# Strassen's seven products for 17 of the 22 pairs of a feed-forward sublayer, in a one-core fp32 block

## The chip, the core and the metric

The kernel runs on one core of a Trainium2 chip, in a single launch. The metric is the device time of that launch in microseconds (us). TensorE (PE in the profile) does the matrix products, VectorE (DVE) and ScalarE (ACT) the elementwise work, GpSimd (POOL) a little of it, and SyncE (SP) issues the DMAs. TensorE's clock has two levels, 1.2 and 2.4 GHz; the profile shows the granted one as a share of the upper.

## The reference

A block of three sublayers on 512 tokens of width 1024, in fp32: a feed-forward sublayer, a mixer of pooling and state-space parts, and a second feed-forward sublayer. Each normalizes its input, modulates it by vectors made from `c`, and adds its gated result to `x`. The change is in the second feed-forward sublayer, whose reference is, cut to what matters (`D_FF` is 2816):

```
def swiglu(h, w_in, w_out):
    a, b = jnp.split(h @ w_in, 2, axis=-1)
    return (jax.nn.silu(a) * b) @ w_out

h = modulate(rmsnorm(x, norm_g[layer, 2]), shift[:, 2], scale[:, 2])
x = x + FFN_RES_WEIGHT * gate[:, 2, None, :] * swiglu(h, ffn2_in[layer], ffn2_out[layer])
return rmsnorm(x, final_g)
```

## The kernel before

**Precision.** An fp32 operand is held as two fp32r tiles, a high part `hi` (a cast) and the rest `lo` (source minus `hi`). A product of two operands is three matmuls into one PSUM bank: hi by hi, hi by lo, lo by hi (`mm3`, L310 to L312). Activations lie with features on the 128 partitions and the 512 tokens along the free dimension, so an operand `h` of 1024 features is 8 such tiles, k = 0 to 7.

**Weights.** They stream from HBM in units of 128 x 1024 (512 KB). For each unit `Weights.load` has SP issue a DMA into a tile `w_raw` (RAW = 3 of them), ScalarE casts it to `w_hi` (L121) and VectorE subtracts to get `w_lo` (L124), in rings of RING = 5 tiles. `fill` asks for the splits of AHEAD = 3 units beyond the one in use. So a cast takes a buffer that TensorE has just finished with, the subtraction follows the cast, and a `w_raw` tile is free for the next DMA after the subtraction.

**A feed-forward sublayer.** The 2816 hidden features are 22 pairs: pair i is the 128 features i of `a` and the 128 of `b`. `pair` makes both products, 8 k each, 512 tokens wide: 48 matmuls of 512 columns. `glu` then takes silu of the first on ScalarE (L524), multiplies by the second on VectorE (L526), and `split` makes the hi and lo tiles (L323 on ScalarE, L325 on VectorE). The pairs come in portions, (0, 8), (8, 16) and (16, 22); after each portion the 8 output products (128 output features each, over the portion's pairs as k) are run and added to `x` by VectorE (`add_out`, L443). Of the last portion two output products are 512 wide and the other six are done in two halves of 256 tokens (`out_halves`), so that the final norm can begin on one half. The first two pairs are made in halves too (`in_halves`). After the last pair come the out products and the final norm.

**Order.** TensorE's order is the program's order, written by hand. The Tile scheduler orders the other engines within the dependencies, and each engine then runs its instructions strictly in the order that it was given. PSUM has 8 banks of 512 fp32, all from one pool, and a wait for a bank is for the whole tile.

**The modulation vectors.** Rows of `w_ada` (512 KB each, tile `row`, 4 of them) are loaded and reduced on VectorE in the first feed-forward sublayer and its start, L391 and L402.

Of the kernel before, what the change touches and what calls it, by code (L numbers as in the profile page):

```python
# [8 lines left out]
F32 = mybir.dt.float32  # L9
# [8 lines left out]
HT = 256  # L18
KD = 8
NPAIR = 22  # L20
PORTIONS = ((0, 8), (8, 16), (16, 22))
NHEAD = 24
NG = 4
NCHK = 4
EPS = 1e-5
NSTART = 4
# [12 lines left out]
WARM = 24  # L39
WARM1 = 7  # L40
# [42 lines left out]
class Weights:  # L83


    def __init__(self, nc, pool, units, big):
        self.nc, self.pool, self.units, self.big = nc, pool, units, big
        self.raw, self.split = [], []
        self.first, self.ring = [0], [0]
        for _, count, _, extra in units:  # L90
            self.first.append(self.first[-1] + count)
            self.ring.append(self.ring[-1] + (not extra))
        self.at = self.done = 0
        self.unit = -1
        self.auto = False

    def load(self, upto):
        while len(self.raw) < min(upto, len(self.units)):
            ap, count, width, _ = self.units[len(self.raw)]
            raw = self.pool.tile([P, KD * P], F32, name="w_raw", tag="w_raw", bufs=RAW)  # L100
            self.nc.sync.dma_start(out=raw[:, :count * width], in_=ap)
            self.raw.append(raw)

    def ensure(self, upto, between=None):
        nc = self.nc
        while len(self.split) < min(upto, len(self.units)):
            i = len(self.split)
            _, count, width, extra = self.units[i]
            self.load(i + 1)
            raw, self.raw[i] = self.raw[i], None  # L110
            parts = []
            step = NT if extra else KD * P
            for c in range(0, count * width, step):
                n = min(step, count * width - c)
                if extra:
# [4 lines left out]
                r = raw[:, c:c + n]  # L120
                nc.scalar.copy(out=hi[:, :n], in_=r)  # L121
                if between:
                    between()
                nc.vector.tensor_tensor(out=lo[:, :n], in0=r, in1=hi[:, :n].bitcast(F32), op=ALU.subtract)  # L124
                parts += [(hi[:, j:j + width], lo[:, j:j + width]) for j in range(0, n, width)]
            self.split.append(parts)

    def fill(self, more=0):

        if not self.auto:  # L130
            return
        used = max(u for u in range(len(self.units) + 1) if self.first[u] <= self.done)
        want = min(self.unit + 1 + AHEAD + more, len(self.units))
        while len(self.split) < want and self.ring[len(self.split) + 1] - self.ring[used] <= RING:
            self.ensure(len(self.split) + 1)
        self.load(min(self.unit + AHEAD + RAW + more, len(self.split) + RAW))

    def next(self, hold=False):

# [96 lines left out]
class Block:  # L236
# [25 lines left out]

    def plan(self):
        a = self.a
        u = [(a["w1s"][k], 2 * NSTART, P, False) for k in range(KD)]
# [7 lines left out]
        def ffn(f, first):  # L273
            for pi, (p0, p1) in enumerate(PORTIONS):
                for t in range(2 * max(p0, first), 2 * p1):
                    u.append((a["ffn%d_in" % f][t], KD, P, False))
                stream(a["ffn%d_out%d" % (f, pi)])

        def halves(ap):
            u.extend((ap[i], KD, P, True) for i in range(4))  # L280

        ffn(1, NSTART)
# [7 lines left out]
        ffn(2, 2)  # L290
        return u

    @staticmethod
    def mixer_order():
# [6 lines left out]
                + [("outB", m) for m in range(MLATE)])  # L301


    def mm3(self, ps, w, act, sl, first, last):
# [5 lines left out]
        T.matmul(o, lhsT=hi, rhs=ahi[:, s], start=first, stop=False)  # L310
        T.matmul(o, lhsT=hi, rhs=alo[:, s], start=False, stop=False)  # L311
        T.matmul(o, lhsT=lo, rhs=ahi[:, s], start=False, stop=last)  # L312

    def product(self, ps, ws, acts, sl=FULL, mid=None):
        for k, act in enumerate(acts):
            if mid:
                mid(k / len(acts))
            self.mm3(ps, ws[k] if ws else self.W.next(), act, sl, k == 0, k == len(acts) - 1)

    def split(self, src, hi, lo, sl=FULL, pool=False):  # L320
        s = slice(*sl)
# [63 lines left out]
        self.accumulate(acc[:, s], q)  # L385


    def ada_load(self, j, k):

        w = self.sb.tile([P, KD * P], F32, name="row", tag="row", bufs=NROW)  # L390
        self.nc.sync.dma_start(out=w, in_=self.a["ada"][j, k])  # L391
        return w

    def ada_sum(self, j, k, w):

# [9 lines left out]
    def ada_rest(self):  # L405

        steps = [(j, k) for j in (2, 4, 3, 5, 7, 6, 8) for k in range(KD)]
        ws = []
        for i, (j, k) in enumerate(steps):
            ws += [self.ada_load(*t) for t in steps[len(ws):i + NROW]]  # L410
            self.ada_sum(j, k, ws[i])
            yield

# [119 lines left out]
        self.product(pb, None, h)  # L533
        self.glu(pa, pb, FULL, g)

    def ffn(self, h, gs, j, gate, norm, late, spread, pumps=(0, 0)):
        for pi, (p0, p1) in enumerate(PORTIONS):
            if pi:
                gs = {i: self.new_act() for i in range(p0, p1)}
            for i in range(max(p0, j), p1):  # L540
                self.pair(h, gs[i])
                self.pump(pumps[0])
            acts = [gs[i] for i in range(p0, p1)]
            last = pi == len(PORTIONS) - 1
            for m in range(late if last else KD):
                self.out_full(m, acts, gate, last)()
                self.pump(pumps[1])
            if last:
                self.pump(1000)
                norm = norm()  # L550
                for m in range(late):
                    norm.scale(m)
                self.out_halves(range(late, KD), acts, gate, norm, spread)


    def start(self):
# [4 lines left out]
    def first_pairs(self):  # L561
# [33 lines left out]

        def load(k):
            if k < KD:
                rows[k] = [self.ada_load(j, k) for j in (1, 0)]
            self.W.load(k + 1)

        for k in range(2):
# [57 lines left out]
        pss = [self.bank() for _ in range(2 * NSTART)]  # L659
        T = nc.tensor  # L660
        for k in range(KD):
            load(k + 2)
            ws = self.W.take(2 * NSTART)
            if k == 0:
                for n, (a, b) in enumerate(((0, 0), (1, 0), (0, 1))):
                    for w, p in zip(ws, pss):
# [9 lines left out]
                self.W.ensure(k + 4)  # L676
        self.W.auto = True
        a = self.a
        gs = {j: self.new_act() for j in range(*PORTIONS[0])}
        for j in range(NSTART):  # L680
# [365 lines left out]
def arrange(inputs):  # L1046
# [61 lines left out]
```

## Time and profile before

| | |
|---|---|
| median of 3 runs | 1138.57 us (1135.80 to 1139.15) |
| the profiled execution | 1137.97 us |
| its span, first to last instruction | 1136.2 us |
| mean granted TensorE clock | 0.996 |
| TensorE busy | 1126.4 us, 99% |
| VectorE busy | 635.6 us, 56% |
| ScalarE busy | 391.2 us, 34% |
| GpSimd busy | 117.3 us, 10% |
| DMA moved | 140.61 MB, 124 GB/s over the span |

The chain of waits is followed back from the last instruction; an engine that holds nearly all of it sets the time. The second feed-forward sublayer runs from about 764 us to the end; pairs 2 to 21 with their output products lie between 780 and 1097 us. A busy share tells how full an engine is, but not whether it hands over late: that is read from single instructions, by their start, their length and what ended the idle time before them. Matmuls are pipelined, so the pace of a stream is the distance of their starts, not the length shown for one.

### The profile page before, as it was taken

The numbers are of one execution on the slowest core, as the hardware profiler recorded it, in microseconds if no ns is written. First come the engines' busy times: TensorE is split into PE (matmuls) and PEld (weight loads), VectorE is DVE, ScalarE is ACT, GpSimd is POOL, SyncE is SP. The second block draws the span as 40 slices with busy tenths as digits, with TensorE's granted clock in tenths as the row PEclk, the third lists the DMA queues.
The fourth block names the chain that finished last, engine by engine and source line by source line (L and its number), as shares of the span: only waits on it lengthen the run. The fifth ranks groups of instructions, "written<-read, shape, count | busy, mean of one in ns | idle before, by whom it ended". The sixth has DMA issues, their size and how long they took to land.

```text
span 1136.2 us, 14273 instructions
## 1 busy us (share of the span) xinstructions
PE 1126.4 (99%) x5708; PEld 937.9 (83%) x5708; DVE 635.6 (56%) x969; ACT 391.2 (34%) x632; POOL 117.3 (10%) x122
## 2 busy tenths in 40 slices
PE   8999999999999999999999999999999999999997
PEld 8888888888888988888888878899888888888887
DVE  6998887333335747778777685563333333333334
ACT  4442122221224534444454452443221222212232
POOL 0000000000000410122302660121000000000011
PEclk8999999999999999999999999999999999999999
DMA  8898986332234302121213123420332223323302
GB/s 323 305 324 319 328 324 250 93 93 93 92 93 132 98 32 90 60 88 62 75 56 89 42 75 93 148 94 21 97 102 97 93 93 93 93 94 94 101 28 74
DMA packets 39954, 140.61 MB, mean 124 GB/s; under 512 B 4432, under 2 KB 5840, under 8 KB 39888
## 3 DMA queue, kind: packets, MB, share of 16 engines
q1 hardware_dynamic: 39888, 139.71, 37.0%
q8 instruction: 44, 0.72, 0.3%
q14 instruction: 22, 0.18, 0.0%
HBM read 137.60 MB, written 2.10 MB: 123 GB/s over the span
## 4 chain that ended last, share of the span: by engine, by line
PE 98%; DMA 1%; DVE 1%; SPq 0%; issue 0%; DVEq 0%
PE ps_mm L311 24%; PE ps_mm L310 24%; PE ps_mm L312 24%; PE ps_t L311 6%; PE ps_t L312 6%; PE ps_t L310 6%; PE ps_y L887 1%; PE ps_mm L373 1%; PE ps_t L881 1%; PE ps_y L906 1%; PE ps_mm L350 1%; DMA row<-in_ada_dram 1%; PE ps_mm L667 1%; PE ps_t L849 0%; PE ps_t L854 0%; PE ps_t L852 0%
## 5 line engine op out<-in xcount | busy, mean ns | idle before, releaser
L310 PE MATMUL ps_mm<-big,w_hi 128*128 128x512 f32 (+1 forms) x1198 | 451.8, 377 | 0.0
L311 PE MATMUL ps_mm<-big,w_hi 128*128 128x512 f32 (+1 forms) x1198 | 450.1, 376 | 0.0
L312 PE MATMUL ps_mm<-big,w_lo 128*128 128x512 f32 (+1 forms) x1198 | 450.0, 376 | 0.0
L121 ACT CAST w_hi<-w_raw 128x1024 fp32r<-128x1024 f32 x176 | 185.0, 1052 | 515.2 <-PE ps_mm L311 341.4
L124 DVE TENSOR_TENSOR w_lo<-w_raw,w_hi 128x1024 fp32r<-128x1024 f32 x176 | 220.2, 1252 | 169.4 <-ACT w_hi L121 159.4
L310 PEld LDWEIGHTS ps_mm<-big,w_hi 128*128 128x128 f32 x1198 | 225.1, 188 | 46.9 <-issue 2.9
L311 PEld LDWEIGHTS ps_mm<-big,w_hi 128*128 128x128 f32 x1198 | 225.5, 188 | 45.2 <-issue 0.7
L312 PEld LDWEIGHTS ps_mm<-big,w_lo 128*128 128x128 f32 x1198 | 224.9, 188 | 42.7
L311 PE MATMUL ps_t<-big,w_hi 128*128 128x512 f32 x304 | 120.2, 395 | 0.0
L312 PE MATMUL ps_t<-big,w_lo 128*128 128x512 f32 x304 | 120.1, 395 | 0.0
L443 DVE SCALAR_TENSOR_TENSOR x<-ps_mm,mod,x 128x512 f32<-128x512 f32 (+1 forms) x79 | 51.0, 647 | 122.6 <-PE ps_mm L312 122.6
L310 PE MATMUL ps_t<-big,w_hi 128*128 128x512 f32 x304 | 119.0, 391 | 0.0
L329 POOL TENSOR_TENSOR sacc<-sacc,sq 128x256 f32<-128x256 f32 (+1 forms) x30 | 28.6, 953 | 729.4 <-ACT sq L384 399.5
L526 DVE TENSOR_TENSOR tmp<-tmp,ps_t 128x512 f32<-128x512 f32 x38 | 26.1, 687 | 112.9 <-PE ps_t L312 112.9
L310 PEld LDWEIGHTS ps_t<-big,w_hi 128*128 128x128 f32 x304 | 57.0, 188 | 14.0
L311 PEld LDWEIGHTS ps_t<-big,w_hi 128*128 128x128 f32 x304 | 57.0, 188 | 13.9
L312 PEld LDWEIGHTS ps_t<-big,w_lo 128*128 128x128 f32 x304 | 57.1, 188 | 12.7
L799 DVE SCALAR_TENSOR_TENSOR big<-ps_mm,vec,big 128x511 f32<-128x511 f32 (+2 forms) x60 | 44.6, 744 | 2.2 <-ACT big L797 1.3
L402 DVE CUSTOM_DVE_ANT_0 row<-row,cb,vec 128x1024 f32<-128x1024 f32 x32 | 40.3, 1279 | 2.7 <-DMA row<-in_ada_dram 2.7
L323 ACT CAST big<-tmp 128x512 fp32r<-128x512 f32 (+1 forms) x66 | 36.4, 554 | 2.5 <-DVE tmp L526 2.0
L310 PE MATMUL ps_mm<-big 128*128 128x256 f32 x128 | 36.5, 285 | 0.0
L311 PE MATMUL ps_mm<-big 128*128 128x256 f32 x128 | 36.2, 283 | 0.0
(170 smaller groups left out, 909.7 us busy)
## 6 DMA issues: line engine op xcount, KB each, us to landing
w_raw<-in_ffn_in_dram SPq DMA_DIRECT2D x76, 512.0 KB, 3.5
row<-in_ada_dram SPq DMA_DIRECT2D x72, 512.0 KB, 5.6
w_raw<-in_ffn_out_dram SPq DMA_DIRECT2D x44, 512.0 KB, 3.7
w_raw<-in_w_in_dram SPq DMA_DIRECT2D x32, 512.0 KB, 3.5
w_raw<-in_w_outB_dram SPq DMA_DIRECT2D x10, 512.0 KB, 3.4
w_raw<-in_w1s_dram SPq DMA_DIRECT2D x8, 512.0 KB, 6.6
w_raw<-in_w_outA_dram SPq DMA_DIRECT2D x6, 512.0 KB, 3.7
x<-in_x_dram SPq DMA_DIRECT2D x4, 512.0 KB, 5.3
```

What stands on the lines that cost most here:

```text
L121: nc.scalar.copy(out=hi[:, :n], in_=r)
L124: nc.vector.tensor_tensor(out=lo[:, :n], in0=r, in1=hi[:, :n].bitcast(F32), op=ALU.subtract)
L310: T.matmul(o, lhsT=hi, rhs=ahi[:, s], start=first, stop=False)
L311: T.matmul(o, lhsT=hi, rhs=alo[:, s], start=False, stop=False)
L312: T.matmul(o, lhsT=lo, rhs=ahi[:, s], start=False, stop=last)
L323: self.nc.scalar.copy(out=hi[:, s], in_=src[:, :n])
L329: self.nc.gpsimd.tensor_tensor(out=acc, in0=acc, in1=q, op=ALU.add)
L350: self.nc.tensor.matmul(ps[:, at + j:at + j + 1], lhsT=acc[:, c * P - c0:(c + 1) * P - c0], rhs=self.ones[:, 0:1], start=i == 0, stop=i == ...
L402: self.nc.vector.tensor_tensor_reduce(out=w, in0=w, in1=self.cb, scale=scale, scalar=bias, op0=ALU.mult, op1=ALU.add, accum_out=out)
L443: self.nc.vector.scalar_tensor_tensor(out=xs, in0=ps[:, :n], scalar=self.mod[:, gate, m:m + 1], in1=xs, op0=ALU.mult, op1=ALU.add)
L526: nc.vector.tensor_tensor(out=g32, in0=sa, in1=pb[:, :n], op=ALU.mult)
L799: V.scalar_tensor_tensor(out=acc[:, s:], in0=ps[:, :NT - s], scalar=tap(3 - s), in1=acc[:, s:], op0=ALU.mult, op1=ALU.add)
```

## The change

For pairs 5 to 21 of the second feed-forward sublayer the two products are made together, by a scheme with seven products in place of eight. The operand is cut in four: tokens 0 to 255 and 256 to 511 (A and B), and k = 0 to 3 and 4 to 7 (low and up). The weights of a pair are cut by k in the same way, and by `a` and `b`. Seven products of four k by 256 columns, of sums of these quarters, give the four quarter results after additions and subtractions. Such a pair (`quad`) is 84 matmuls of 256 columns.

- The sums of activations are made once, by `combine`, during pairs 2 to 4, which stay plain.
- The sums of weights are made on VectorE for each pair (`part`, L134, L135, L139), in place in a new tile `row` of 128 x 5 x 512, of which there are two. The four weight quarters come in two DMAs (768 and 256 KB, L121 and L122); what comes from the sums are three units of 1024 (U0, U1, U2) and one of 512 (U3), cast by L167 and subtracted by L170.
- A quad's products stand in nine places s1 to s9: x, y, x again, z, out product 1, x, out product 2, z, x. y and z are the two halves of one bank. ScalarE copies partial sums out (L448, L454, L456), VectorE adds what comes later (L450, L462, L466).
- The portions become (0, 4), (4, 8), (8, 12), (12, 16), (16, 22), and the output products of one portion are woven between the pairs of the next: two to a pair, and 1, 1, 2, 1, 1, 2 in the last six.
- RAW goes from 3 to 2, loads may run up to 8 units ahead, and the ada rows come two to a `row` tile.

The diff, cut to its core:

```
+PORTIONS = {1: ((0, 8), (8, 16), (16, 22)), 2: ((0, 4), (4, 8), (8, 12), (12, 16), (16, 22))}
+FIRST = {1: 4, 2: 2}
+QUADS = {1: NPAIR, 2: 5}
+WOVEN = {1: False, 2: True}
-RAW = 3
+RAW = 2
-NROW = 4
+NROW = 2
+LOADS = 8
...
+            if quad:
+                raw = self.last = self.row()
+                self.nc.sync.dma_start(out=raw[:, 2:5].rearrange("p s n -> p (s n)"), in_=ap[:, NT:])
+                self.nc.sync.dma_start(out=raw[:, 0], in_=ap[:, :NT])
...
+    def part(self, raw, kind):
+        V = self.nc.vector
+        if kind == 0:
+            return raw[:, 2::2]
+        if kind == 1:
+            V.tensor_tensor(out=raw[:, 1:4:2], in0=raw[:, 0:3:2], in1=raw[:, 3:4].broadcast_to([P, 2, NT]), op=ALU.add)
+            V.tensor_tensor(out=raw[:, 2], in0=raw[:, 1], in1=raw[:, 2], op=ALU.add)
+            return raw[:, 1:3]
+        if kind == 2:
+            return raw[:, 0:4:3]
+        V.tensor_tensor(out=raw[:, 4], in0=raw[:, 2], in1=raw[:, 4], op=ALU.add)
+        return raw[:, 4:5]
...
+    def combine(self, h):
...
+        for k in range(n):
+            wa, wb, t, u = (self.tmp() for _ in range(4))
+            for w, (hi, lo) in ((wa, h[k]), (wb, h[k + n])):
+                add(w, hi.bitcast(F32), lo.bitcast(F32), ALU.add)
+            add(t[:, la], wa[:, la], wa[:, lb], ALU.subtract)
+            less(t[:, lb], t[:, la], wb[:, lb])
+            self.t12[k] = self.new_act()
+            self.split(t, *self.t12[k])
...
+    def quad(self, h, g, outs):
...
+        x, yz = self.bank(), self.bank("t")
+        y, z = yz[:, :HT], yz[:, HT:]
+        one, two = self.tmp(), self.tmp()
+        la, lb = slice(*HALF_A), slice(*HALF_B)
+        ws = W.take(2 * n, hold=True)
+        block(x, ws[:n], low, True)
+        S.copy(out=one[:, la], in_=x[:, la])
+        block(y, ws[n:], [(act, HALF_A) for act in up], True)
+        V.tensor_tensor(out=one[:, la], in0=one[:, la], in1=y, op=ALU.add)
+        W.release(2 * n)
+        ws = W.take(2 * n, hold=True)
+        block(x, ws[n:], t2, False)
+        S.copy(out=one[:, lb], in_=x[:, la])
+        block(z, ws[:n], t1, True)
+        S.copy(out=two[:, lb], in_=z)
+        W.release(2 * n)
+        outs = outs()
+        outs[0]()
+        wb = W.take(2 * n, hold=True)
+        block(x, wb[n:], self.t3, False)
+        V.tensor_tensor(out=two[:, lb], in0=two[:, lb], in1=x[:, la], op=ALU.add)
+        outs[1]()
+        W.fill()
+        block(z, W.take(n, hold=True), [(act, HALF_B) for act in up], False)
+        V.tensor_tensor(out=one[:, lb], in0=one[:, lb], in1=z, op=ALU.add)
+        block(x, wb[:n], t4, False)
+        W.release(3 * n)
+        S.activation(out=one, in_=one, func=AF.Silu)
+        for src, c in ((two, lb), (x, la)):
+            V.scalar_tensor_tensor(out=two[:, c], in0=src[:, c], scalar=-1.0, in1=one[:, c], op0=ALU.mult, op1=ALU.mult)
+        self.split(two, *g)
...
+        self.bg = self.combine(norms[2].h)
+        self.ffn(2, norms[2].h, gs, 8, lambda: final, LATE2, SPREAD3, (2, 0))
```

On VectorE a stretch of the second portion of before reads as follows; a pair has two subtractions for its weights, its multiplication (L526) and its split (L325), and output products follow after the portion, each with its addition (L443) and a subtraction:

```order
L124 TENSOR_TENSOR w_lo<-w_raw,w_hi 128x1024
L526 TENSOR_TENSOR tmp<-tmp,ps_t 128x512
L124 TENSOR_TENSOR w_lo<-w_raw,w_hi 128x1024
L325 TENSOR_TENSOR big<-tmp,big 128x512
L443 SCALAR_TENSOR_TENSOR x<-ps_mm,mod,x 128x512
```

After the change, twelve of the sixteen VectorE rows of the step from one pair to the next (here from pair 7 to pair 8) are below; L466 and the two L471 end pair 7, the first two L170 are U2 and U3 of pair 8, L450 belongs to pair 8, then come U0 and U1 of pair 9 with L135 and L139, and L134 makes the first sums of pair 10:

```order
L466 TENSOR_TENSOR tmp<-tmp,ps_t 128x256
L170 TENSOR_TENSOR w_lo<-row,w_hi 128x1024
L471 SCALAR_TENSOR_TENSOR tmp<-tmp 128x256
L471 SCALAR_TENSOR_TENSOR tmp<-ps_mm,tmp 128x256
L170 TENSOR_TENSOR w_lo<-row,w_hi 128x512
L479 TENSOR_TENSOR big<-tmp,big 128x512
L450 TENSOR_TENSOR tmp<-tmp,ps_t 128x256
L170 TENSOR_TENSOR w_lo<-row,w_hi 128x1024
L135 TENSOR_TENSOR row<-row 128x512
L139 TENSOR_TENSOR row<-row 128x512
L170 TENSOR_TENSOR w_lo<-row,w_hi 128x1024
L134 TENSOR_TENSOR row<-row 128x2x512
```

The four rows after these are the output addition L601, L462, a second L601 and the subtraction of the out weights; then the same sixteen rows come again for the next pair. L450, which reads y, now stands behind the previous pair's L471, the subtraction of U3 and the split L479.

On TensorE, the border between the two products of pair 5 of before, with the waits of its matmuls (ps_mm is the bank of the first product, ps_t that of the second; Activation and DVE are the engines whose signal is waited for):

```order
L310 MATMUL ps_mm<-big,w_hi 128x512
L311 MATMUL ps_mm<-big,w_hi 128x512
L312 MATMUL ps_mm<-big,w_lo 128x512
L310 MATMUL ps_t<-big,w_hi 128x512 [waits Activation_49]
L311 MATMUL ps_t<-big,w_hi 128x512
L312 MATMUL ps_t<-big,w_lo 128x512 [waits DVE_49]
```

After the change the border from s3 to s4 of a quad, where z (in ps_t) follows x (in ps_mm):

```order
L381 MATMUL ps_mm<-big,w_hi 128x256
L382 MATMUL ps_mm<-big,w_hi 128x256
L383 MATMUL ps_mm<-big,w_lo 128x256
L381 MATMUL ps_t<-big,w_hi 128x256 [waits DVE_49]
L382 MATMUL ps_t<-big,w_hi 128x256
L383 MATMUL ps_t<-big,w_lo 128x256
L381 MATMUL ps_t<-big,w_hi 128x256
```

The waits of before are for the cast and the subtraction of the weights of the second product; that of the quad is for VectorE's L450, which reads the other half of the same bank.

## Rows read from the trace of the kernel before

**Rows 1.** The page: engines' busy time, and the chain that ended last.

```profile
PE 1126.4 (99%) x5708; PEld 937.9 (83%) x5708; DVE 635.6 (56%) x969; ACT 391.2 (34%) x632; POOL 117.3 (10%) x122
...
PE 98%; DMA 1%; DVE 1%; SPq 0%; issue 0%; DVEq 0%
```

**Rows 2.** Busy time by stretch: PE, PEld, DVE, ACT, POOL, clock, DMA share, GB/s.

```profile
0.00:120.00 120.00, 117.12 (x524) 96.40 (x525) 104.28 (x156) 44.82 (x57) 0.73 (x6) 0.97 0.89 320
...
900.00:1050.00 150.00, 150.00 (x651) 121.86 (x650) 51.96 (x55) 38.44 (x46) 0.00 (x0) 1.00 0.30 95
...
1098.00:1114.00 16.00, 16.00 (x131) 15.69 (x130) 4.88 (x8) 4.07 (x10) 4.96 (x6) 1.00 0.01 2
```

**Rows 3.** Groups by shape, 784 to 1097 us: busy, mean ns, idle before, releaser.

```profile
L124 DVE TENSOR_TENSOR w_lo<-w_raw,w_hi 128x1024 fp32r<-128x1024 f32 x56 | 68.6, 1225 | 81.5 <-ACT w_hi L121 77.0
...
L121 ACT CAST w_hi<-w_raw 128x1024 fp32r<-128x1024 f32 x57 | 59.9, 1051 | 231.1 <-PE ps_mm L311 151.0 <-issue 64.1 <-PE ps_t L311 16.0
...
L526 DVE TENSOR_TENSOR tmp<-tmp,ps_t 128x512 f32<-128x512 f32 x20 | 13.7, 687 | 70.2 <-PE ps_t L312 70.2
...
L325 DVE TENSOR_TENSOR big<-tmp,big 128x512 fp32r<-128x512 f32 x20 | 13.7, 683 | 0.0
...
L443 DVE SCALAR_TENSOR_TENSOR x<-ps_mm,mod,x 128x512 f32<-128x512 f32 x17 | 12.7, 750 | 55.3 <-PE ps_mm L312 55.3
...
L323 ACT CAST big<-tmp 128x512 fp32r<-128x512 f32 x20 | 12.4, 622 | 0.0
...
L524 ACT ACTIVATE tmp<-ps_mm 128x512 f32<-128x512 f32 x20 | 11.8, 592 | 0.0
```

**Rows 4.** TensorE in a pair: start us, us, engine, line, operation.

```profile
785.54 0.39 PE L310 MATMUL ps_mm<-big,w_hi 128*128 128x512 f32 x1
...
787.62 0.39 PE L310 MATMUL ps_t<-big,w_hi 128*128 128x512 f32 x1
```

**Rows 5.** TensorE's 256-column matmuls, and one weight load.

```profile
765.20 0.28 PE L310 MATMUL ps_mm<-big 128*128 128x256 f32 x1
...
780.56 0.28 PE L312 MATMUL ps_mm<-big 128*128 128x256 f32 x1
...
1099.85 0.28 PE L312 MATMUL ps_mm<-big,w_lo 128*128 128x256 f32 x1
...
1100.20 0.19 PEld L310 LDWEIGHTS ps_mm<-big,w_hi 128*128 128x128 f32 x1
...
1113.98 0.28 PE L312 MATMUL ps_mm<-big,w_lo 128*128 128x256 f32 x1
```

**Rows 6.** Groups by shape, 560 to 1136 us, 256 columns wide.

```profile
L443 DVE SCALAR_TENSOR_TENSOR x<-ps_mm,mod,x 128x256 f32<-128x256 f32 x18 | 8.7, 481 | 19.8 <-PE ps_mm L312 19.8
...
L526 DVE TENSOR_TENSOR tmp<-tmp,ps_mm 128x256 f32<-128x256 f32 x4 | 1.7, 420 | 8.7 <-ACT tmp L524 6.6 <-issue 2.1
...
L524 ACT ACTIVATE tmp<-ps_mm 128x256 f32<-128x256 f32 x4 | 1.5, 386 | 6.7 <-PE ps_mm L312 6.7
```

**Rows 7.** Single instructions: handing over between engines, and two in a row.

```profile
785.76 0.40 PE L311 MATMUL ps_mm<-big,w_hi 128*128 128x512 f32 x1
...
786.20 1.05 ACT L121 CAST w_hi<-w_raw 128x1024 fp32r<-128x1024 f32 x1 [4.39 <-PE ps_mm L311]
...
787.28 1.23 DVE L124 TENSOR_TENSOR w_lo<-w_raw,w_hi 128x1024 fp32r<-128x1024 f32 x1 [5.02 <-ACT w_hi L121]
...
903.76 1.22 DVE L124 TENSOR_TENSOR w_lo<-w_raw,w_hi 128x1024 fp32r<-128x1024 f32 x1
...
904.91 0.68 DVE L325 TENSOR_TENSOR big<-tmp,big 128x512 fp32r<-128x512 f32 x1
```

**Rows 8.** DMA issues, time to landing; last the row tile, 0 to 120 us.

```profile
w_raw<-in_ffn_in_dram SPq DMA_DIRECT2D x76, 512.0 KB, 3.5
...
out_dram<-big SPq DMA_DIRECT2D x4, 256.0 KB, 2.4
...
DMA to landing us min/median/max: 3.4/5.5/9.5
```

More of the change, by code (lines that the diff above doesn't have):

```diff
@@ L25 @@
 EPS = 1e-5
-NSTART = 4
 LATE1 = 2
@@ L107, in ensure @@
             i = len(self.split)
-            _, count, width, extra = self.units[i]
+            _, count, width, kind = self.units[i]
             self.load(i + 1)
             raw, self.raw[i] = self.raw[i], None
+            if kind in (True, False) and type(kind) is bool:
+                self.out[False] -= 1
+            else:
+                self.out[True] -= kind == 3
+                raw = self.part(raw, kind)
             parts = []
-            step = NT if extra else KD * P
+            step = NT if kind is True else KD * P
             for c in range(0, count * width, step):
                 n = min(step, count * width - c)
-                if extra:
+                if kind is True:
                     hi, lo = self.big(F32R), self.big(F32R)
@@ L135, in fill @@
             self.ensure(len(self.split) + 1)
-        self.load(min(self.unit + AHEAD + RAW + more, len(self.split) + RAW))
+        self.load(min(self.unit + AHEAD + LOADS + more, len(self.split) + LOADS))
     def next(self, hold=False):
@@ L264, in plan @@
         a = self.a
-        u = [(a["w1s"][k], 2 * NSTART, P, False) for k in range(KD)]
+        u = [(a["w1s"][k], 2 * FIRST[1], P, False) for k in range(KD)]
         def stream(ap):
@@ L271, in stream, with ffn @@
                 u.append((ap[:, t * P:e * P], e - t, P, False))
[L273 to L277, printed above, removed]
+        def ffn(f):
+            w, out = a["ffn%d_in" % f], "ffn%d_out%d"
+            for i, outs in self.steps(f):
+                if i is None:
+                    stream(a[out % (f, outs[0][0])])
+                    continue
+                ts = []
+                if outs:
+                    pi = outs[0][0]
+                    n = PORTIONS[f][pi][1] - PORTIONS[f][pi][0]
+                    m = outs[0][1]
+                    ts = [(a[out % (f, pi)][:, m * n * P:(m + len(outs)) * n * P], n * len(outs), P, False)]
+                if i < QUADS[f]:
+                    u.extend([(w[2 * i], KD, P, False), (w[2 * i + 1], KD, P, False)] + ts)
+                else:
+                    u.extend([(a["ffn%d_inQ" % f][i - QUADS[f]], KD, P, 0), (None, KD, P, 1)] + ts
+                             + [(None, KD, P, 2), (None, KD // 2, P, 3)])
+            stream(a[out % (f, len(PORTIONS[f]) - 1)])
         def halves(ap):
             u.extend((ap[i], KD, P, True) for i in range(4))
-        ffn(1, NSTART)
+        ffn(1)
         halves(a["w_inH"])
@@ L289, in plan, with steps @@
         halves(a["ffn2_inH"])
-        ffn(2, 2)
+        ffn(2)
         return u
+    @staticmethod
+    def steps(f):
+        for pi, (p0, p1) in enumerate(PORTIONS[f]):
+            pairs = range(max(p0, FIRST[f]), p1)
+            n = len(pairs)
+            for x, i in enumerate(pairs):
+                ms = range(x * KD // n, (x + 1) * KD // n) if pi and WOVEN[f] else ()
+                yield i, [(pi - 1, m) for m in ms]
+            if not WOVEN[f] and pi < len(PORTIONS[f]) - 1:
+                yield None, [(pi, m) for m in range(KD)]
     @staticmethod
@@ L301, in mixer_order, with mm3 @@
                 + [("outB", m) for m in range(MLATE)])
-    def mm3(self, ps, w, act, sl, first, last):
+    def mm3(self, ps, w, act, sl, first, last, again=False):
         hi, lo = w
@@ L318, in product, with add, less @@
             self.mm3(ps, ws[k] if ws else self.W.next(), act, sl, k == 0, k == len(acts) - 1)
+    def combine(self, h):
+        V = self.nc.vector
+        n = KD // 2
+        la, lb = slice(*HALF_A), slice(*HALF_B)
+        self.t12, self.t3 = [None] * n, [None] * n
+        last = []
+        def add(out, a, b, op):
+            V.tensor_tensor(out=out, in0=a, in1=b, op=op)
+        def less(out, a, b):
+            V.scalar_tensor_tensor(out=out, in0=a, scalar=-1.0, in1=b, op0=ALU.mult, op1=ALU.subtract)
+        for k in range(n):
[6 more added lines that the diff above has]
+            self.split(t, *self.t12[k])
+            if k % 2 == 0:
+                three, four = self.new_act(), self.big()
+            sl = (HALF_A, HALF_B)[k % 2]
+            add(u[:, la], wb[:, lb], wa[:, lb], ALU.subtract)
+            self.split(u, *three, sl)
+            self.t3[k] = three, sl
+            less(four[:, slice(*sl)], t[:, lb], wb[:, la])
+            last.append((four[:, slice(*sl)], h[k]))
+            yield
+        while self.plain:
+            yield
+        for src, act in last:
+            self.split(src, *act, HALF_B)
+        yield
@@ L385, in square_into, with ada_load @@
         self.accumulate(acc[:, s], q)
[L388 to L392, printed above, removed]
+    def ada_load(self, todo):
+        row = self.W.row().rearrange("p s n -> p (s n)")
+        ws = []
+        for i, (j, k) in enumerate(todo):
+            ws.append(row[:, i * KD * P:(i + 1) * KD * P])
+            self.nc.sync.dma_start(out=ws[i], in_=self.a["ada"][j, k])
+        return ws
     def ada_sum(self, j, k, w):
@@ L409, in ada_rest @@
         for i, (j, k) in enumerate(steps):
-            ws += [self.ada_load(*t) for t in steps[len(ws):i + NROW]]
+            while i % 2 == 0 and len(ws) < min(i + 4, len(steps)):
+                ws += self.ada_load(steps[len(ws):len(ws) + 2])
             self.ada_sum(j, k, ws[i])
@@ L534, in pair, with ffn, weights, outs @@
         self.glu(pa, pb, FULL, g)
[L536 to L540, printed above, removed]
+    def ffn(self, f, h, gs, gate, norm, late, spread, pumps=(0, 0)):
+        ports = PORTIONS[f]
+        def weights(todo):
+            return [self.W.take(ports[pi][1] - ports[pi][0], hold=True) for pi, _ in todo]
+        def outs(todo, ws=None):
+            for n, (pi, m) in enumerate(todo):
+                acts = [gs[i] for i in range(*ports[pi])]
+                ps = self.bank()
+                self.product(ps, ws[n] if ws else weights([(pi, m)])[0], acts)
+                self.W.release(len(acts), False)
+                self.add_out(ps, m, FULL, gate, False)
+                self.pump(pumps[1])
+        def halves(todo):
+            ws = weights(todo)
+            return [lambda: outs(todo[:1], ws[:1]), lambda: outs(todo[1:], ws[1:])]
+        self.plain = True
+        for i, todo in self.steps(f):
+            if i is None:
+                outs(todo)
+                continue
+            gs[i] = self.new_act()
+            if i < QUADS[f]:
                 self.pair(h, gs[i])
                 self.pump(pumps[0])
[L543 to L548, printed above, removed]
-                self.pump(1000)
[L550 to L553, printed above, removed]
+                outs(todo)
+                continue
+            if self.plain:
+                self.plain = False
+                self.pump(1000)
+            self.quad(h, gs[i], lambda: halves(todo))
+        acts = [gs[i] for i in range(*ports[-1])]
+        for m in range(late):
+            self.out_full(m, acts, gate, True)()
+            self.pump(pumps[1])
+        self.pump(1000)
+        norm = norm()
+        for m in range(late):
+            norm.scale(m)
+        self.out_halves(range(late, KD), acts, gate, norm, spread)
     def start(self):
@@ L597, in load @@
             if k < KD:
-                rows[k] = [self.ada_load(j, k) for j in (1, 0)]
+                rows[k] = self.ada_load([(1, k), (0, k)])
             self.W.load(k + 1)
@@ L657, in prepare @@
                                                   op0=ALU.add, op1=ALU.subtract)
-        pss = [self.bank() for _ in range(2 * NSTART)]
+        pss = [self.bank() for _ in range(2 * FIRST[1])]
         T = nc.tensor
```

66 lines of the change are left out of this document (46 added, 20 removed).

## The prediction

> **What bounds the kernel now.** I read the page's first part and its chain of waits, then the stretch table of the second feed-forward sublayer, then single instructions. TensorE is busy for 99% of the span and 98% of the chain is TensorE [rows 1]: time is won only by giving it less to do, as long as nothing makes it wait. In the sublayer's stretch that holds without a gap: 150.00 of 150 us at full clock (2.4 GHz), with VectorE at 52 us (35%), ScalarE at 38 and the DMA engines at 0.30 [rows 2]. VectorE and ScalarE wait for TensorE there: the cast of a weight (L121) follows the last read of the buffer it takes, the subtraction (L124) follows the cast [rows 3]. So two questions decide: how fast TensorE runs the new, smaller matmuls, and whether VectorE, which gets twice the work, still hands over in time.
>
> **TensorE's sum.** A pair now is 48 matmuls of 512 columns. From one L310 to the ninth matmul after it pass 2.08 us [rows 4], 0.2311 us each: 11.09 us a pair. A quad is 84 matmuls of 256 columns (seven products, four k, three each). Such matmuls run in two places of before: 120 steps from 1099.85 to 1113.98, 0.1178 each, twelve or more to a bank; and 128 steps from 765.20 to 780.56, 0.1200 each, with a new bank every three [rows 5]. The quad stays twelve matmuls in a bank, so I take 0.1178: 9.89 us. Bounds: 0.1200 gives 10.08, half of a 512-column step gives 9.71. A quad saves 1.20 us (1.01 to 1.38), seventeen save 20.4 us (17.2 to 23.5). The out products keep their matmuls and shapes (528 of k times m, however they are cut); the end of the sublayer is unchanged. A change between widths costs nothing by the rows: a step is as long as the matmul before it.
>
> Each matmul has its own weight load, so 17 x 36 = 612 are added. One takes 0.19 us, longer than the step it has to fit in; yet in the 256-column stretch loads start every 0.12 us beside the matmuls and the pace holds [rows 5]. I cost them at nothing. The Trainium skill ("TensorE: Matmul & The Clock Gate", "The mechanism") says that a weight load overlaps matmuls in flight only where their row groups differ; here all are full height, and the trace speaks against it. By that rule the change would lose (a rival below).
>
> **VectorE's sum.** With two out products woven in, a pair's sixteen VectorE rows are: four subtractions of 1024 (1.225) and two of 512 (0.683, one of them the split), the sum L134, L135 and L139, three additions from PSUM, two multiplications, two output additions (0.750) [rows 3, 6]. The sums are not in the trace: L134 has 1024 elements out, so I take the 1024-wide subtraction's 1.225; L135 and L139 have 512: 0.687. Their two-slot and broadcast reads could double that; the lower bound is the same 1024 at twice the 256-wide speed, about 0.8. PSUM additions of 256: 0.42; multiplications: 0.48 [rows 6]. Sum: 4.90 + 1.37 + 1.23 + 1.37 + 1.26 + 0.96 + 1.50 = 12.6 us. Such a pair lasts 9.89 + 2 x 12 x 0.2311 = 15.44 us on TensorE (16.64 before), so VectorE is at 82%; before it had 3 x 1.225 + 0.687 + 0.683 + 0.750 = 5.8 us for the same work. Throughput suffices; order has to be looked at.
>
> **The one tight wait.** Take t = 0 at a pair's first matmul; the nine blocks s1 to s9 are in the order of the code. y and z share a bank, and the fourth block (z, 36 x 0.1178 = 4.24 us) waits for VectorE's read of y, L450. VectorE runs in its fixed order, so L450 stands behind the previous pair's end. From the rows a matmul's end reaches ScalarE or VectorE about 0.04 us later, a cast's end VectorE 0.03 later, and back-to-back VectorE instructions start 0.07 before the listed end [rows 7]. U2's cast takes the buffer that the last-but-one matmul of s8 reads: it runs from -1.33 to -0.28. L466 ends at -0.20, U2's subtraction at 0.98, silu (0.592) at 0.43. The two L471 run to 1.79, U3's subtraction of 512 to 2.39, the split's cast (0.622) from 1.91 to 2.53, L479 to 3.25, and L450 from 3.18 to 3.60. TensorE would start z at 4.24: slack 0.64 us. I cost the wait at nothing; if the cover goes, every microsecond counts seventeen times.
>
> The other waits have more. x's second use (s3, 2.83) needs the ScalarE copy L448, done at 2.01. The next pair's U0 is subtracted by 5.2, L135 and L139 at 5.8 and 6.6, U1's at 8.2, L134 at 9.3, L462 at 10.3; its waiter s9 starts at 14.03. With one out product (pairs 16, 17, 19, 20) s9 starts at 11.26 and L462 ends near 10.95; in pair 17, where the next out weights are 1024 wide, at 11.5: 0.3 us lost. The sums of activations (combine, four times two additions and a split of 512 and five steps of 256, 4.3 us each) fall into pairs 2 to 4, where VectorE has little else; the queue is clear when pair 5 wants L450.
>
> **Loads.** Bytes are the same, one row of 1 MB in two DMAs for two of 512 KB. 512 KB land in 3.5 us, 256 KB in 2.4 [rows 8]: 1.1 per 256 KB, so 1 MB in about 5.7 (up to 9.5, the longest of a row while DMA was at 0.89 [rows 2, 8]). A row tile is free after U3's subtraction (2.39); the new row lands near 8.1 and L134, which waits for both of its DMAs, gets to it at the same time. Behind L134 stand the output addition and L462: it may come 3.7 us later before s9 notices. On SP nothing but these DMAs and the out weights queue. RAW 3 to 2 and the ada rows two to a tile move loads in the first 120 us, where VectorE has 16 us to spare and DMA is at 0.89 [rows 2]; the weights of the first pairs are asked for as soon as before, within some us of slack. I take 0.3, bounds 0 and 2.
>
> **Total.** The profiled execution took 1137.97 us (span 1136.2 and 1.8 around it), 0.6 under the median of 1138.57. 1137.97 - 20.4 + 0.3 + 0.3 = 1118.2, so 1118.
>
> **Rivals.**
> (a) z waits in every pair. The chain above is six VectorE steps, two ScalarE steps and a buffer rule. If U2's cast gets its buffer only after s9 (another order of buffers than I read), it is 1.41 us later, the slack of 0.64 goes and 0.77 us stall: 17 x 0.77 = 13.1, time 1131. The same comes from steps 15% longer and some more latency each, with a smaller price (0.1 to 0.5 us a pair, 1120 to 1126). For it: fourteen waits in a row, and 1024-wide sums that no row shows. Against it: each step is a measured length. The order guards the whole bank: z's columns are not y's. The Trainium skill ("PSUM — Partial Sum Buffer", "PSUM bank collisions raise a hardware error") has that rule, to guard by bank and not by address; no run here shows a collision. With a guard by address z would not wait for L450, and (a) would lose most of its chance.
> (b) Slower: the row's landing blocks VectorE at L134. L134 heads a strict queue; L462 behind it needs 2.25 us, so s9 is late once a row takes more than 9.2 us (11.74 less the issue at 2.5), and the whole saving of a pair is gone at 10.4. If two DMAs of a row take twice the 5.5 of the loaded stage, 11.0, the twelve pairs with two out products and a row to load lose 1.8 each, three with one (limit 6.4, since more stands between) lose 4.6 each: 35 us, time 1153. For it: the loads now come as a burst of 1 MB. Against: the DMA share stays at 0.30, where no landing is near that. At about half of this it would end within 0.3% of before.
> (c) Slower: weight loads are not hidden at 256 columns in a quad. 612 x 0.188 = 115 us more, time 1233; it decides from 0.033 us exposed per added load. This is the skill's row-group rule above; rows 5 speak plainly against it.
> (d) Nothing is won: L134, L135 and L139 are twice as long as taken (2.6 us more per pair, VectorE at 98%), with L462 and L466 late: about the 1.2 us a pair that was saved, 1138.
>
> **How the numbers follow.** The forecast (TensorE stays the bound, 1114 to 1122): 0.62. (a) in either size: 0.24. (b) 0.07, (c) 0.01, (d) 0.06. Within 0.3% (3.4 us) is about what a measurement cannot tell from no change. Faster: the forecast and (a), 0.86; same: most of (d), 0.06; slower: (b), (c) and what is left of (d), 0.08. The range for 8 in 10 starts at 1113, where the best pace of the smaller matmuls puts it with the runs' own spread, and ends at 1131, taking in (a).
>
> **What would show it.** In the profile after: 256-column steps of 0.118 in the quads; a quad pair with two out products of 15.4 us and one with one of 12.7; TensorE at 99% with 612 more matmuls; VectorE near 80% of the stretch; L134 near 1.2 us; L450 ending some 0.6 us before z's first matmul. Gaps of TensorE ahead of the fourth block mean (a); ahead of s9, with L134 waiting for DMA, (b); a step near 0.3 us (c); sums of over 2 us (d). The prediction is wrong if the pairs before the quads, or the first 120 us, are longer than before by more than 2 us.

## The result and the profile after

The changed kernel takes 1117.7 us (median of 4 runs, 1116.12 to 1119.57), the kernel before 1137.9: a ratio of 0.9825, 95% interval 0.9803 to 0.9847. The forecast was 1118.0, faster. The profiled execution took 1117.88 us for a span of 1116.1, 20.1 us less than that of before.

| stretch of the span | before | after |
|---|---|---|
| up to the first 512-column matmul after the halves of pairs 0 and 1 | 780.68 | 780.10 |
| from there to the first 256-column matmul of the last out products | 318.94 | 299.59 |
| from there to the end | 36.58 | 36.41 |

19.35 of the 20.1 us lie in the stretch that the change touches; 0.58 ahead of it and 0.17 behind it are within the spread of the runs.

The page of the changed kernel, engines' busy time and then the chain that ended last:

```profile
PE 1105.1 (99%) x6320; PEld 952.8 (85%) x6320; DVE 752.3 (67%) x1176; ACT 441.8 (40%) x731; POOL 118.4 (11%) x122
...
PE 97%; DVE 2%; DMA 0%; issue 0%; ACT 0%; DVEq 0%; SPq 0%; ACTq 0%
```

Against [rows 1]: 612 more matmuls, 21 us less TensorE, 117 us more VectorE, and TensorE still holds the chain. The same stretch as in [rows 2] (PE, PEld, DVE, ACT, POOL, clock, DMA share, GB/s):

```profile
900.00:1050.00 150.00, 149.71 (x1068) 140.25 (x1067) 116.08 (x160) 68.08 (x103) 0.00 (x0) 1.00 0.31 98
```

VectorE went from 35% to 77% of the stretch; TensorE idles 0.29 us of 150, at full clock; DMA is at 0.31 (0.30 before).

TensorE from pair 9 to pair 10: the first matmul of pair 9, and the border from s3 to s4 in both:

```profile
880.79 0.28 PE L381 MATMUL ps_mm<-big,w_hi 128*128 128x256 f32 x1
...
884.92 0.28 PE L383 MATMUL ps_mm<-big,w_lo 128*128 128x256 f32 x1
885.03 0.28 PE L381 MATMUL ps_t<-big,w_hi 128*128 128x256 f32 x1
...
900.50 0.28 PE L381 MATMUL ps_t<-big,w_hi 128*128 128x256 f32 x1
```

36 matmuls take 885.03 - 880.79 = 4.24 us, 0.1178 each as in [rows 5]. The pitch from z to z, 15.47, is 0.03 over the 15.44 of the sum. VectorE from the end of pair 8 into pair 9 (start, length, line; a bracket tells idle time and what ended it):

```profile
880.21 0.41 DVE L466 TENSOR_TENSOR tmp<-tmp,ps_t 128x256 f32<-128x256 f32 x1
880.59 1.23 DVE L170 TENSOR_TENSOR w_lo<-row,w_hi 128x1024 fp32r<-128x1024 f32 x1
881.73 0.42 DVE L471 SCALAR_TENSOR_TENSOR tmp<-tmp 128x256 f32<-128x256 f32 x1
882.07 0.42 DVE L471 SCALAR_TENSOR_TENSOR tmp<-ps_mm,tmp 128x256 f32<-128x256 f32 x1
882.40 0.68 DVE L170 TENSOR_TENSOR w_lo<-row,w_hi 128x512 fp32r<-128x512 f32 x1
883.33 0.69 DVE L479 TENSOR_TENSOR big<-tmp,big 128x512 fp32r<-128x512 f32 x1 [0.25 <-ACT big L477]
883.94 0.41 DVE L450 TENSOR_TENSOR tmp<-tmp,ps_t 128x256 f32<-128x256 f32 x1
```

L450 ends at 884.35, z starts at 885.03: slack 0.68 us (forecast 0.64), and it is 0.67 to 0.73 in all 17 pairs. The new sums, by shape in 784 to 1080 us, and the only gap of TensorE there:

```profile
L381 PE MATMUL ps_mm<-big,w_hi 128*128 128x256 f32 x273 | 76.9, 282 | 0.3 <-DVE tmp L462 0.3
...
L134 DVE TENSOR_TENSOR row<-row 128x1024 f32<-128x1024 f32 x15 | 18.3, 1218 | 0.3 <-DMA row<-in_ffn_inQ_dram 0.3
...
L135 DVE TENSOR_TENSOR row<-row 128x512 f32<-128x512 f32 x17 | 11.8, 693 | 0.6
L139 DVE TENSOR_TENSOR row<-row 128x512 f32<-128x512 f32 x17 | 11.8, 692 | 0.5
```

The two-slot and broadcast forms cost what the plain ones of [rows 3] do, and L134 waits 0.3 us for rows in this stretch (two of its 17 stand far ahead of it, at 195 and 200 us, in the first feed-forward sublayer). A row's two DMAs, issued 0.38 us apart, land in:

```profile
row<-in_ffn_inQ_dram SPq DMA_DIRECT2D x17, 768.0 KB, 4.6
...
row<-in_ffn_inQ_dram SPq DMA_DIRECT2D x17, 256.0 KB, 4.8
```

### The profile page after: what moved, and what is told of

Same layout as the page of the kernel before. It is cut to its first block, busy times and chain, and to the rows that moved or that the text cites. A ratio compares the mean times of both kernels' runs of the same rounds, so it can differ in the third digit from the quotient of the medians.

```text
span 1116.1 us, 15784 instructions
## 1 busy us (share of the span) xinstructions
PE 1105.1 (99%) x6320; PEld 952.8 (85%) x6320; DVE 752.3 (67%) x1176; ACT 441.8 (40%) x731; POOL 118.4 (11%) x122
## 4 chain that ended last, share of the span: by engine, by line
PE 97%; DVE 2%; DMA 0%; issue 0%; ACT 0%; DVEq 0%; SPq 0%; ACTq 0%
PE ps_mm L381 24%; PE ps_mm L383 24%; PE ps_mm L382 24%; PE ps_t L381 6%; PE ps_t L383 6%; PE ps_t L382 6%; PE ps_y L1071 1%; PE ps_mm L504 1%; PE ps_t L1065 1%; PE ps_y L1090 1%; PE ps_mm L527 1%; PE ps_t L1033 1%; PE ps_t L1038 1%; PE ps_t L1036 1%; DMA x<-in_x_dram 0%; DVE w_lo L170 0%
## 5 line engine op out<-in xcount | busy, mean ns | idle before, releaser
L381 PE MATMUL ps_mm<-big,w_hi 128*128 128x512 f32 (+1 forms) x1334 | 477.8, 358 | 0.3 <-DVE tmp L462 0.3
L382 PE MATMUL ps_mm<-big,w_hi 128*128 128x512 f32 (+1 forms) x1334 | 471.9, 354 | 0.4 <-DVE big L840 0.4
L167 ACT CAST w_hi<-w_raw 128x1024 fp32r<-128x1024 f32 (+1 forms) x144 | 149.8, 1040 | 368.3 <-PE ps_mm L382 201.1
L382 PEld LDWEIGHTS ps_mm<-big,w_hi 128*128 128x128 f32 x1334 | 252.5, 189 | 38.8 <-DVE big L840 0.9
L381 PEld LDWEIGHTS ps_mm<-big,w_hi 128*128 128x128 f32 x1334 | 251.2, 188 | 38.9 <-issue 2.9
L170 DVE TENSOR_TENSOR w_lo<-w_raw,w_hi 128x1024 fp32r<-128x1024 f32 (+1 forms) x144 | 179.1, 1244 | 91.9 <-ACT w_hi L167 85.9
L601 DVE SCALAR_TENSOR_TENSOR x<-ps_mm,mod,x 128x512 f32<-128x512 f32 (+1 forms) x95 | 62.9, 663 | 90.9 <-PE ps_mm L383 90.8
L383 PE MATMUL ps_t<-big,w_lo 128*128 128x256 f32 (+1 forms) x372 | 124.1, 334 | 0.0
L381 PE MATMUL ps_t<-big,w_hi 128*128 128x256 f32 (+1 forms) x372 | 124.1, 334 | 0.0
L382 PE MATMUL ps_t<-big,w_hi 128*128 128x256 f32 (+1 forms) x372 | 123.5, 332 | 0.0
L170 DVE TENSOR_TENSOR w_lo<-row,w_hi 128x1024 fp32r<-128x1024 f32 x68 | 74.1, 1089 | 17.8 <-ACT w_hi L167 17.8
L167 ACT CAST w_hi<-row 128x1024 fp32r<-128x1024 f32 x68 | 63.8, 939 | 53.5 <-DVE row L135 24.5
L382 PEld LDWEIGHTS ps_t<-big,w_hi 128*128 128x128 f32 x372 | 70.7, 190 | 8.4
L381 PEld LDWEIGHTS ps_t<-big,w_hi 128*128 128x128 f32 x372 | 70.0, 188 | 7.7
L479 DVE TENSOR_TENSOR big<-tmp,big 128x512 fp32r<-128x512 f32 (+1 forms) x58 | 38.8, 676 | 6.6 <-ACT big L477 6.3
```

The costliest lines, as they stand in the source:

```text
L167: nc.scalar.copy(out=h, in_=r)
L170: nc.vector.tensor_tensor(out=l, in0=r, in1=h.bitcast(F32), op=ALU.subtract)
L381: T.matmul(o, lhsT=hi, rhs=ahi[:, s], start=first, stop=False, skip_group_check=again)
L382: T.matmul(o, lhsT=hi, rhs=alo[:, s], start=False, stop=False, skip_group_check=again)
L383: T.matmul(o, lhsT=lo, rhs=ahi[:, s], start=False, stop=last, skip_group_check=again)
L479: eng.tensor_tensor(out=lo[:, s], in0=src[:, :n], in1=hi[:, s].bitcast(F32), op=ALU.subtract)
```

## Experiments

Theory: TensorE's shorter work is the whole saving, and all the rest is hidden with 0.7 us to spare at one wait. Rivals: part of it came from the portions and loads; VectorE's work costs something; the wait is not one for the bank.

**Everything but the quads.**

```
-QUADS = {1: NPAIR, 2: 5}
+QUADS = {1: NPAIR, 2: NPAIR}
...
-        self.bg = self.combine(norms[2].h)
+        self.bg = iter(())
```

> The portions of four, the woven out products, two w_raw tiles and the ada rows two to a tile, but all pairs plain (no quads, no sums). My theory (the saving is the quads' 17 x 1.20 us alone): as before, 1137 to 1139. Rival (portions, weaving or the loads' order gave part of it): under 1135.

Measured: 1139.12 us, ratio to before 1.0016 (1.0004 to 1.0028). With plain pairs, portions of four, woven out products and the other loads give nothing; they cost 0.0 to 0.3%. Without the quads there is no saving. That the quads need the weaving is another matter (below, out products not woven).

**Sums of weights left out.** U1, U3 and the second half of U2 are taken from unsummed quarters, which have the same sizes.

```
-            V.tensor_tensor(out=raw[:, 1:4:2], in0=raw[:, 0:3:2], in1=raw[:, 3:4].broadcast_to([P, 2, NT]), op=ALU.add)
-            V.tensor_tensor(out=raw[:, 2], in0=raw[:, 1], in1=raw[:, 2], op=ALU.add)
-            return raw[:, 1:3]
+            return raw[:, 2:4]
...
-        V.tensor_tensor(out=raw[:, 4], in0=raw[:, 2], in1=raw[:, 4], op=ALU.add)
```

> Leaves the sums of weights out (L134, L135, L139; the products take unsummed quarters). My theory (VectorE's added work is hidden, TensorE is the bound): 0.3 us less at most, the one gap in pair 17: 1117 to 1118. Rival (the sums cost something on the path, part of the distance to the ideal saving of 20.4): 1112 or less.

Measured: 1118.08 us (0.9824, 0.9805 to 0.9844), the same as the change. The 42 us that L134, L135 and L139 take in the stretch are hidden but for one place: TensorE's only gap (pair 17, below) is gone with them. The stretch of [rows 2] in this kernel:

```profile
900.00:1050.00 150.00, 150.00 (x1066) 140.42 (x1065) 91.64 (x129) 67.97 (x103) 0.00 (x0) 1.00 0.30 96
```

That gap is too short to be seen in the times.

**Sums of weights made twice**, the second time on top of the first, in place.

```
+            for _ in range(2):
+                V.tensor_tensor(out=raw[:, 1:4:2], in0=raw[:, 0:3:2], in1=raw[:, 3:4].broadcast_to([P, 2, NT]), op=ALU.add)
+                V.tensor_tensor(out=raw[:, 2], in0=raw[:, 1], in1=raw[:, 2], op=ALU.add)
...
+        for _ in range(2):
+            V.tensor_tensor(out=raw[:, 4], in0=raw[:, 2], in1=raw[:, 4], op=ALU.add)
```

> Makes each sum of weights twice, VectorE at 15.1 of 15.44 us in a pair with two out products and 14.4 of 12.67 in one with one. My rival (d) had 1.2 us per pair for this, 1138. Refined by the order: pairs with two out products keep some 0.2 us of slack and lose nothing, the three or four with one lose about 1.7 each: 1122 to 1127. If the first is right, gaps of TensorE stand in every pair.

Measured: 1118.9 us (0.9837, 0.9814 to 0.986). Less than either expectation. VectorE in the pairs with two out products (822 to 976 us), and in 992 to 1062, where the pairs with one stand:

```profile
822.00:976.00 154.00, 154.00 (x1077) 143.32 (x1076) 140.28 (x190) 69.63 (x99) 0.00 (x0) 1.00 0.31 100
992.00:1062.00 70.00, 69.58 (x517) 65.98 (x516) 65.99 (x94) 35.40 (x53) 0.00 (x0) 1.00 0.28 91
```

TensorE does not idle at all with VectorE at 91%: U1's subtraction and the second L139 now stand behind L462, in the 2.3 us that VectorE had idled ahead of the second output addition, and L452 (the read of y in this kernel) still ends 0.67 us before z. At 94% the slack sinks to 0.05 in one pair and TensorE loses 0.4 us there:

```profile
1020.61 0.39 PE L383 MATMUL ps_t<-big,w_hi 128*128 128x256 f32 x1 [0.42 <-DVE tmp L452]
```

My 1.7 us for each pair with one out product were wrong: I had added up work per pair, but pair 18 with two lies between, pair 20 has no L134, and (argued, not shown) weights that come 2 us later are still early for TensorE. Rival (d) falls: twice the sums cost 1.2 us by the medians, which is within the spread of the runs, and not 20.

**y read four more times**, with the bank shared and with z in its own.

```
         V.tensor_tensor(out=one[:, la], in0=one[:, la], in1=y, op=ALU.add)
+        for _ in range(4):
+            V.tensor_tensor(out=two[:, la], in0=one[:, la], in1=y, op=ALU.add)
```

and in the second kernel also

```
-        y, z = yz[:, :HT], yz[:, HT:]
+        y, z = yz[:, :HT], self.bank("t")[:, :HT]
```

> After y is read by L450, VectorE reads it four more times into a scratch half; the order puts these reads between the subtraction of U0, L135 and L139, so the last one ends about 7.5 us after the pair's start, where z's first matmul is due at 4.24. My theory (z waits for the last reader of its bank, with 0.68 us of slack now): TensorE stalls about 3.3 us ahead of the fourth block in each of the 17 pairs, 56 us, time near 1174. Rival (z waits only for its own columns, so the reads cost VectorE's time alone, 1.4 us per pair that is hidden but in the four pairs with one out product): 1118 to 1124.

> The same four more reads of y, with z in a bank of its own. My theory: the stall ahead of the fourth block is gone, and VectorE (about 14.0 of 15.44 us) stays hidden in the pairs with two out products; in the four with one, L462 comes up to 1.4 us later, some 4 us in all: 1118 to 1124. Rival (what costs is VectorE's added work or its order, not the shared bank): as long as the run with the shared bank, near 1174.

Measured: 1200.44 us shared (ratio 1.0559, 1.0527 to 1.0591), 1119.35 with its own bank (0.9839, 0.9821 to 0.9858). The same reads cost 82.7 us, or 1.7, which is hardly more than the spread of the runs. In both kernels VectorE has the four reads at the same places of its order. Waits of the two kernels for the read, first shared (total, times, longest), then own bank (ScalarE's only, TensorE has none):

```profile
PEld ps_t L381 <- DVE tmp L452: 55.4, 17, 3.3
PE ps_t L381 <- DVE tmp L452: 51.9, 17, 3.1
```

```profile
ACT w_hi L167 <- DVE tmp L452: 0.3, 1, 0.3
```

So z does wait for the whole bank, and the stall is about the 3.3 us expected. 56 us were expected in all, though, and 82.7 came. The stretch around one stall, shared bank (columns as in [rows 2]; then TensorE's matmuls at its end):

```profile
925.00:928.70 3.70, 0.62 (x6) 0.41 (x4) 3.68 (x8) 0.59 (x2) 0.00 (x0) 1.00 0.64 254
928.70:932.00 3.30, 3.27 (x14) 3.18 (x15) 1.12 (x1) 0.66 (x1) 0.00 (x0) 0.54 0.00 0
932.00:936.00 4.00, 4.00 (x24) 3.47 (x24) 1.98 (x2) 0.66 (x2) 0.00 (x0) 0.95 0.00 0
```

```profile
928.73 0.40 PE L381 MATMUL ps_t<-big,w_hi 128*128 128x256 f32 x1 [3.11 <-DVE tmp L452]
928.95 0.39 PE L382 MATMUL ps_t<-big,w_hi 128*128 128x256 f32 x1
...
931.05 0.41 PE L383 MATMUL ps_t<-big,w_lo 128*128 128x256 f32 x1
931.27 0.63 PE L381 MATMUL ps_mm<-big,w_hi 128*128 128x512 f32 x1
931.70 0.63 PE L382 MATMUL ps_mm<-big,w_hi 128*128 128x512 f32 x1
```

After 3.1 us of idleness the granted clock is at 0.54, nearly the lower of its two levels: z's twelve matmuls take 931.27 - 928.73 = 2.54 us and not 1.41, and the next two or three of 512 columns take 0.43 and not 0.23. That is some 1.6 us more for this stall. By the distances of z's starts, 16 of the 17 stalls cost 1.4 to 1.7 us in this way; the second, as long as the others, cost 0.1, and the granted clock stayed at 1.00 around it (847 to 855 us). That makes 26 us; with the 55 of the stalls it is 81 of the 82.

**Each row loaded twice into the same tile.**

```
-                self.nc.sync.dma_start(out=raw[:, 2:5].rearrange("p s n -> p (s n)"), in_=ap[:, NT:])
-                self.nc.sync.dma_start(out=raw[:, 0], in_=ap[:, :NT])
+                for _ in range(2):
+                    self.nc.sync.dma_start(out=raw[:, 2:5].rearrange("p s n -> p (s n)"), in_=ap[:, NT:])
+                    self.nc.sync.dma_start(out=raw[:, 0], in_=ap[:, :NT])
```

> Each quad's row is loaded twice into the same tile, so it lands after about 9.5 us and not 4.7. My limits: L462 is late for the last block once a row takes more than 9.2 us in pairs with two out products and 6.4 in those with one. So twelve pairs lose up to 0.5 each and three lose about 3: 1122 to 1137. Rival (loads are far enough ahead in any case): 1118. Rival (b) at full size would need over 11 us: 1153.

Measured: 1121.72 us (0.9864, 0.9839 to 0.9888), 4.0 more than the change, just under the range expected. One row, first its issue on SP, then VectorE around the sum that waits for it (L135 here; L463 is the L462 of the change):

```profile
913.98 0.33 SPq L122 DMA_DIRECT2D row<-in_ffn_inQ_dram  x1
```

```profile
921.11 0.42 DVE L463 TENSOR_TENSOR tmp<-tmp,ps_mm 128x256 f32<-128x256 f32 x1 [0.73 <-PE ps_mm L384]
924.19 1.23 DVE L135 TENSOR_TENSOR row<-row 128x1024 f32<-128x1024 f32 x1 [2.67 <-DMA row<-in_ffn_inQ_dram]
```

The row is complete 10.2 us after its issue. By my limits (9.2 and 6.4) that would lose 12 x 1.0 + 3 x 3.8 = 23 us. It loses 4: the scheduler, given the longer load, put the sum behind L463, where it had stood ahead of L462. The wait no longer blocks the addition that s9 wants; what is late is the chain behind it, by about as much as its slack: TensorE waits 2.0 us in this stretch, three times for L451 and twice for L463, which is about 3 us by the distances of its starts; the profiled execution is 3.1 longer than that of the change. The mechanism of rival (b) is real (VectorE waits 30.6 us for rows), its price was taken for an order that does not stay.

**Out products not woven.**

```
-WOVEN = {1: False, 2: True}
+WOVEN = {1: False, 2: False}
```

> Quads as in the change, but the out products after their portions, not between the pairs. TensorE's work is the same. My theory (weaving gives VectorE and ScalarE the 5.5 us per pair that they need behind a quad): a quad alone is 9.89 us of TensorE and about 9.9 us of VectorE in chains with ScalarE, so it stretches by 0.5 to 1.5 us in most pairs: 1125 to 1140, with TensorE waiting ahead of blocks for L450 and weights. Rival (VectorE's queue is filled ahead anyway, during the stretches of out products): 1118 to 1121.

Measured: 1132.14 us (0.9954, 0.9939 to 0.997); the profiled execution, 1128.40, was the fastest of eight. There the quads follow each other every 10.2 us where their matmuls need 9.9 (the first matmul of z, twice, then TensorE's waits at the portions' borders: total, times, longest):

```profile
913.95 0.28 PE L381 MATMUL ps_t<-big,w_hi 128*128 128x256 f32 x1
...
924.14 0.28 PE L381 MATMUL ps_t<-big,w_hi 128*128 128x256 f32 x1
```

```profile
PE ps_mm L381 <- ACT big L477: 3.4, 4, 1.2
PE ps_mm L382 <- DVE big L479: 2.6, 5, 0.7
```

An out product right behind the last quad of its portion waits for that quad's split: 0.9 to 2.4 us at a border by the distance of starts, 8.5 at the five of them (the first stands behind plain pairs). The time is in the range that I expected, but not for my reason: a quad stretches by 0.3 us and not by 0.5 to 1.5, and the borders, which I had left out, cost more than that. By the medians weaving is worth 14 us of the 20 (by the profiled executions 10.5; what the other executions lose beyond it no trace shows): without it the same TensorE work is held up by its own handovers. With plain pairs weaving gave nothing, so it is worth its 14 us to the quads alone.

**The same in the first feed-forward sublayer**, for its pairs 15 to 21, so 24 quads in all.

```
-PORTIONS = {1: ((0, 8), (8, 16), (16, 22)), 2: ((0, 4), (4, 8), (8, 12), (12, 16), (16, 22))}
+PORTIONS = {1: ((0, 4), (4, 8), (8, 12), (12, 16), (16, 22)), 2: ((0, 4), (4, 8), (8, 12), (12, 16), (16, 22))}
...
-QUADS = {1: NPAIR, 2: 5}
-WOVEN = {1: False, 2: True}
+QUADS = {1: 15, 2: 5}
+WOVEN = {1: True, 2: True}
...
-PUMPS = (3, 1)
+PUMPS = (4, 1)
...
+        self.bg = chain(self.bg, self.combine(h))
         self.ffn(1, h, gs, 2, lambda: norm(1), LATE1, SPREAD1, PUMPS)
```

> The same portions and weaving in the first feed-forward sublayer, with quads for its pairs 15 to 21 and the ada sums pumped a little faster before them. If the gain per quad is TensorE's own, 7 x 1.20 = 8.4 us less: 1109 to 1111. Rival (the first sublayer's VectorE, with ada sums of 1.28 us each, and its DMA of about 280 GB/s have no room): 1117 or more.

Measured: 1110.91 us (0.9764, 0.9744 to 0.9783): 6.8 less than the change, of the 8.4 that seven times 1.2 make, and the fastest version here. In the stretch with the new quads TensorE idles 0.29 of 80 us:

```profile
250.00:330.00 80.00, 79.71 (x582) 75.16 (x581) 65.87 (x93) 37.05 (x58) 0.00 (x0) 1.00 0.34 109
```

Two waits of s9 for its addition (this one, ending at 289.90, and one ending at 331.30) take 1.1 us by the distances of starts; the first sublayer is done 7.0 us earlier than in the change.

## Why the prediction was right

- **TensorE's sum.** 0.1178 us a step, 17 quads, 20.4 us less: measured 0.1178, 15.47 instead of 15.44 us a pair, 1.17 saved per pair, 19.9 in all. The pace came from 256-column matmuls elsewhere in the same kernel, with a new weight load each, and it carried over. Leaving the quads out gives it all back.
- **Weight loads.** Still 0.19 us each and beside the matmuls at 0.1178 a step, so rival (c) falls. The row-group rule of the Trainium skill ("TensorE: Matmul & The Clock Gate", "The mechanism") is not what this trace shows.
- **The tight wait.** Slack 0.64 forecast, 0.68 measured. The wait was shown to be one for the bank; with more reads of y it costs the stall that the argument gave, 3.3 us a pair, and half as much again through the clock. Rival (a) was a real mechanism, 0.7 us away, and did not come. The Trainium skill's rule ("PSUM — Partial Sum Buffer", "PSUM bank collisions raise a hardware error") to guard a bank as a whole is what the order does; whether a collision would happen without it no run here shows.
- **The small term.** 0.3 us was set for pair 17, where L462 would be late for s9. TensorE's only gap in the stretch is there:

```profile
1013.01 0.41 DVE L462 TENSOR_TENSOR tmp<-tmp,ps_mm 128x256 f32<-128x256 f32 x1
...
1013.48 0.38 PE L381 MATMUL ps_mm<-big,w_hi 128*128 128x256 f32 x1 [0.29 <-DVE tmp L462]
```

  By the distance of TensorE's starts it costs 0.55 us: the pitch from z to z around it is 13.24, and 12.69 for the other pairs with one out product.
- **What evened out.** That 1118.2 came so near to 1117.9 is in part luck. The quads saved 0.5 us less than the sum and pair 17 cost 0.25 more, while the part ahead of the quads came out 0.9 under its term and the end 0.2 under; the last two are within the spread of the runs. The mechanism and its main term hold without that.
- **Mis-sized, without effect on the time.** A row is complete about 5.2 us after its first issue (4.8 for the second DMA, which is issued 0.38 later), not 5.7: the 768 KB take the 4.6 that their size tells, and the other 256 KB come in beside them. The L471 take 0.42, not the 0.48 of an addition with a per-partition factor. And (b) and (d) were priced too high, (d) by far: both took VectorE's work per pair as if nothing could move, while in both experiments the scheduler put work behind L462.
- **Left open.** The term of 0.3 us for the first 120 us: the stage ended 0.58 us earlier, which is within the spread; nothing was run for it.

## What to carry to other kernels

Where TensorE holds the chain without a gap, a cut in its columns was worth its steps (19.35 of 20.4 us here), at a pace read from the same width elsewhere in the trace, as long as each handover kept some slack; so find the shortest slack by laying out one period from the rows, and mind that a bank is waited for as a whole. Put other work of the same engine between the shortened stages (here out products), since a shorter stage leaves less time for its own handovers. A busy share per period is no price for added work: at 91% it was free.

## What the runs showed of the hardware

A stall of TensorE of 3.1 us, once in every 16 to 20 us, cost about 1.6 us beyond itself in 16 of 17 cases: in the one shown the matmuls behind it ran at a granted clock of 0.54 until the pace was back some 3.7 us later. Waits of up to 1.2 us in the unwoven kernel left its clock at 1.00 (860 to 940 and 990 to 1010 us). VectorE's addition over two strided slots with a broadcast operand took 1.218 us for 1024 elements, as long as a plain subtraction (1.225).
